# Cache copies as quarters behind the input projection's loads, weight sums behind additions, and a residual put into PSUM

## The chip, the core and the metric

The kernel runs on one core of a Trainium2 chip. TensorE (PE) multiplies matrices and loads its weights on a path of its own (PEld in the profile); VectorE (DVE) and ScalarE (ACT) work on tiles in SBUF and PSUM; GpSimd (POOL) and SyncE (SP) mostly start DMAs here. Each engine has a queue of its own and takes it in order; engines wait for each other by semaphores. The metric is the time of one execution on the device in microseconds (us), lower is better.

## What is computed

One layer of a hybrid decoder, for a prompt of 512 tokens and 8 single sample tokens, 520 columns in all (260 + 260, each half 256 prompt columns and 4 samples), width 1024, float32:

```python
u = rmsnorm(x, g_norm1)
qa, ka, va, qb, kb, vb, rb, glr, ga, gb = split(u @ w_in)        # input projection
oa = dilated window attention(qa, ka, va)                        # prompt, and samples against their caches
ob = gated linear attention(qb, kb, vb, gate(glr))
mix = sigmoid(ga) * (oa @ w_pa) + sigmoid(gb) * (gated ob @ w_pb)
h = x + mix @ w_o
f = square(relu(rmsnorm(h, g_norm2) @ w_up))                     # width 4096
y = rmsnorm(h + f @ w_down, g_final)
```

The new caches of the sample group are outputs too: the old ones, moved by one row, with the new keys and values behind them. The kernel copies the old caches unchanged from DRAM to DRAM; the host puts the new row behind.

## The kernel before

Every product has three passes, since PE multiplies in a rounded format: high part of the weights by high part of the data, high by low, low by high. A weight panel (128 output columns, 1024 inputs, 512 KB) is loaded by SP into a tile raw, ACT rounds it to whi (L138), and DVE subtracts to get wlo (L139); split_piece does both for four k-tiles at a time. While panel i runs, panel i + 1 is split and panel i + 2 loaded.

The program is one straight line. Outside the FFN, Tile's scheduler orders each engine's queue from dependences and an estimate of when things are ready. In the FFN the order is written out: `act`, `add` and `stt` go through `turn` (L119), which chains every instruction of ACT and DVE behind the last one, matmuls are chained by `behind`, and `load` (L86) chains all loads that SP starts. An instruction that waits there holds up all that stands behind it on its engine.

Stages: input projection (58 panels of w_in, `panel_mms` L272, with attention and linear attention filled in between the matmuls), w_pa, w_pb, w_o, and from L1521 the FFN in four quarters of the hidden width. A quarter is four up pairs and, in the first three, four down pairs; `pair_mm` (L203) does one pair. The last quarter's down product is done panel by panel at the end, in two column ranges, 280 and 240 (L1600 to L1647), each with its final norm.

A pair makes a 2 x 2 block product (two panels, two halves of the columns) by seven products instead of eight, in the manner of Strassen and Winograd: P1, P5, P6, P3, P7, P2, P4, each 12 matmuls of 128 x 260. P1 and P2 use plain weights, P5 and P7 use differences of weights (tile sums, made by a load and an accumulating load of POOL, L114 and L115), P6 and P3 use tile s, which `pair_sums` (L146) makes with two DVE additions from sums and raw, and P4 uses the last quarter block (tile rb, `load_rest`). The data side has sums as well (tiles Th/Tl, FT and the second halves of hh and fh). P1, P6, P7 and P4 add up in one PSUM bank x, P5 and P3 in e; P2 adds to a copy of P1 in a. P4 can therefore start only when DVE has read x after P7.

Which work of the next pair stands where in the queues is set by `lead(i, step)`: step 0 makes the sums s, steps 1 to 3 split weights. The results of a pair go on in the next one: `then` of `up_pair` (L1209) gets the names T0, T1, T2 at the start, after P1 and after P5 of the next pair and makes ReLU, square, split and data sums there. `down_pair` (L1282) adds a pair's results into dd, on DVE (in the first quarter the first ones are ACT copies).

`extras` (L1547) puts small work into the down pairs: the squares of h in the first quarter (reloaded from the DRAM copy Hd), in the second the mean square (r2: four ones-matmuls and rv on DVE at P1 of the first down pair, four reciprocals of 130 columns), in the third dd times rv and then the residual, by an accumulating DMA of POOL from Hd into dd (L1578). `pace` (L339) starts the cache copies on POOL, one of 1024 rows (1 MB) a call, each behind a matmul; there are 42 in self.copies, the last 16 for ca3v.

Of the kernel before, what the change touches and what calls it, by code (L numbers as in the profile page):

```python
# [47 lines left out]
class Build:  # L48
# [114 lines left out]
    def lead(self, i, step):  # L163

        if self.panels[i][1] != PAIR:
            if step in (1, 2):
                self.split_panel(i, (4 * step - 4,))
        elif step == 0:
            self.pair_sums(i)
        else:  # L170
            self.pair_piece(i, *{1: ("P1",), 2: ("P6", "P5"), 3: ("P7",)}[step])

    def split_panel(self, i, parts=(0, 4)):
# [6 lines left out]
        if self.panels[i][1] == PAIR:  # L180
            for step in range(3):
                self.lead(i, step)
            return
# [19 lines left out]
    def pair_mm(self, acts, then):  # L203
# [15 lines left out]
        if before:  # L219
            before("T0")  # L220
        self.load_panel(i + 2)
        for n, o, start, end in seq:
# [11 lines left out]
            if n == "P1":  # L234
                if before:
                    before("T1")
            elif n == "P5":
                if before:
                    before("T2")
                if "P7" not in self.ready[i]:  # L240
                    self.pair_piece(i, "P7")
                self.pair_piece(i, "P4" if first else "P2")
                if pair:
                    self.lead(i + 1, 0)
# [7 lines left out]
            elif n == "P7":  # L252
                if not last:
                    self.lead(i + 1, 2)
# [5 lines left out]
            if n == "P2" and pair and not then(n + " ends"):  # L260
                self.lead(i + 1, 3)
        if pair:
            self.later = lambda n: then(n, a, e, x)
        else:
            for n in ("T0", "T1", "T2"):
                then(n, a, e, x)
# [5 lines left out]
    def panel_mms(self, xh, xl, m, pool=None):  # L272
# [6 lines left out]
        if i + 2 < len(self.panels):  # L279
            self.load_panel(i + 2)  # L280
        if i + 1 < len(self.panels):
# [875 lines left out]
    def up_pair(self, p, work, k, fh, fl, T, copies, rv):  # L1157
# [51 lines left out]
        def then(n, a=None, e=None, x=None):  # L1209
# [27 lines left out]
            elif n == "P2 ends":  # L1237
                return end
# [6 lines left out]
            elif n == "T0":  # L1245
# [15 lines left out]
            elif n == "T1":  # L1261
# [4 lines left out]
                else:  # L1266
                    split(4, v["t"])
                    if T:
                        high(0)
            elif n == "T2" and T:  # L1270
                if end:
                    high(2)
                    self.add(fl[:, k + 4], v["t"], fh[:, k + 4].bitcast(F32), op=ALU.subtract)
                    low(2)
                else:
                    high(1)
                    high(2)
                    for n in range(3):
                        low(n)
        return then  # L1280

    def down_pair(self, k, dd, qd, also):  # L1282
# [14 lines left out]
        def then(n, a=None, e=None, x=None):  # L1297
# [11 lines left out]
            elif n == "P4":  # L1309
                self.pace(1)  # L1310
            elif n == "T0":
                put(1, one, x, -1)
# [3 lines left out]
    def run(self):  # L1316
# [26 lines left out]
        for n in ("a1k", "a1v", "a2k", "a2v", "a3k", "a3v"):  # L1343
# [3 lines left out]
            for x in range(pieces):  # L1347
                f = lambda t: t[x * st:(x + 1) * st].rearrange("(a b) c -> a (b c)", a=16)
                self.copies.append((f(o), f(i)))
        self.rate, self.tiny_rate, self.groups_ready = 0, 2, 1  # L1350
# [125 lines left out]
        with pool("late") as p:  # L1476
# [70 lines left out]
            def extras(qd, k):  # L1547
# [3 lines left out]
                def also(n):  # L1551
# [10 lines left out]
                    elif qd == 1:  # L1562
                        if n == "P1" and k == 0:
# [8 lines left out]
                        elif n == "P4":  # L1572
                            c = slice(65 * k, 65 * k + 130)
                            self.turn("DVE", nc.vector.reciprocal(rv[:, c], rv[:, c]))
                    elif n in ("P4", "T0"):
                        x = k + (n == "T0")
                        self.add(dd[:, x], dd[:, x], rv, op=ALU.mult)
                        nc.gpsimd.dma_start(dd[:, x], Hd[:, x], accum_op=ALU.add)  # L1578
                return also

            for qd in range(4):
                n0 = len(self.panels) - KT
                for k in range(4):
                    if qd == 3 and k == 3:
                        self.wdst[n0] = [p.tile([P, KT, P], F32R, tag="sums", name="lw", bufs=3) for _ in range(2)]
                    if qd + k == 0:
                        self.later = lambda n: (list(self.sums_left), low()) if n == "T1" else None
                    self.pair_mm(acts, self.up_pair(p, work, k, fh, fl, T if qd < 3 else None, k % 2 or qd == 3,
# [11 lines left out]
            for j, cc in enumerate((slice(0, JC), slice(JC, NT))):  # L1600
                n = cc.stop - cc.start
                for k in range(KT):
# [6 lines left out]
                    ps = self.bank("mps")[:, :n]  # L1609
                    for kk in (0, 1, 2, 4, 5, 6, 3, 7):  # L1610
                        for x, (w, u) in enumerate(self.passes(self.split[i], kk, fh, fl)):
                            self.last = nc.tensor.matmul(ps, w, u[:, kk, cc], start=(kk == 0 and x == 0),  # L1612
                                                         stop=(kk == KT - 1 and x == 2))
# [185 lines left out]
```

## Time and profile before

| what | us |
|---|---|
| median of 3 runs (896.15 to 899.48) | 898.85 |
| the profiled execution | 898.83 |
| its span in the profile | 897.1 |
| PE busy | 870.5 |
| DVE busy | 659.1 |
| ACT busy | 473.3 |

The profile is of one execution. A stretch of the trace is named by its start and end in us from the start of the span. "Busy" is the time in which at least one instruction of the engine runs; matmuls overlap, so two that follow each other closely count once. The granted clock is the share of PE's full clock, and the DMA share is the mean busy share of the 16 DMA engines. In the timeline a row has start, length, engine, line, operation, tiles (out<-in) and shapes, and in brackets how long the engine stood idle before and what ended the wait by the trace. Of several things waited for, the one that came last is named, and it can be the wrong one.

### The profile page before, as it was taken

The numbers are of one execution on the slowest core, as the hardware profiler recorded it, in microseconds if no ns is written. First come the engines' busy times: TensorE is split into PE (matmuls) and PEld (weight loads), VectorE is DVE, ScalarE is ACT, GpSimd is POOL, SyncE is SP. The second block draws the span as 40 slices with busy tenths as digits, with TensorE's granted clock in tenths as the row PEclk, the third lists the DMA queues.
The fourth block names the chain that finished last, engine by engine and source line by source line (L and its number), as shares of the span: only waits on it lengthen the run. The fifth ranks groups of instructions, "written<-read, shape, count | busy, mean of one in ns | idle before, by whom it ended". The sixth has DMA issues, their size and how long they took to land.

```text
span 897.1 us, 19539 instructions
## 1 busy us (share of the span) xinstructions
PE 870.5 (97%) x7818; PEld 847.2 (94%) x7818; DVE 659.1 (73%) x1333; ACT 473.3 (53%) x989; POOL 118.8 (13%) x171
## 2 busy tenths in 40 slices
PE   9999999999999999999999999999989998998995
PEld 8999999999999999999999999899989998998995
DVE  6877566775947849695755778977998798887843
ACT  6233424453736545364533558867864585456732
POOL 1110000001200302101001211111111111231000
PEclk9999999999999999999999999999999999999998
DMA  7476465324545534225797967799778877998531
GB/s 256 125 269 206 133 212 200 109 73 147 181 151 171 187 128 142 77 72 195 280 380 285 334 227 210 226 310 317 241 198 236 278 229 211 240 298 291 194 122 69
DMA packets 52323, 184.14 MB, mean 205 GB/s; under 512 B 6588, under 2 KB 11716, under 8 KB 50408
## 3 DMA queue, kind: packets, MB, share of 16 engines
q1 hardware_dynamic: 37432, 104.26, 33.4%
q0 software_dynamic: 14512, 78.14, 29.1%
q8 instruction: 61, 1.00, 0.4%
q10 hardware_dynamic: 288, 0.49, 0.2%
q14 instruction: 30, 0.25, 0.1%
HBM read 167.01 MB, written 56.30 MB: 249 GB/s over the span
## 4 chain that ended last, share of the span: by engine, by line
PE 84%; DMA 5%; DVE 5%; ACT 3%; issue 1%; SPq 0%; DVEq 0%; ACTq 0%; POOLq 0%
PE mps L299 48%; PE mps L227 21%; PE mps L1612 5%; DMA sums<-in_w_up 4%; ACT t L128 1%; PE lev L894 1%; PE mps L465 1%; ACT whi L128 1%; PE sps L640 1%; DVE s L131 1%; DVE fl L131 1%; PE pvp L673 1%; DVE wlo L131 1%; PE gpo L1003 1%; PE gpu L1007 1%
## 5 line engine op out<-in xcount | busy, mean ns | idle before, releaser
L299 PE MATMUL mps<-uh,whi 128*128 128x260 f32 x896 | 255.9, 286 | 0.0
L299 PE MATMUL mps<-ul,whi 128*128 128x260 f32 x896 | 255.8, 286 | 0.0
L299 PE MATMUL mps<-uh,wlo 128*128 128x260 f32 x896 | 255.3, 285 | 0.0
L128 ACT ACTIVATE whi<-raw 128x512 fp32r<-128x512 f32 (+1 forms) x210 | 128.8, 619 | 180.4 <-PE mps L299 146.7
L131 DVE TENSOR_TENSOR wlo<-raw,whi 128x512 fp32r<-128x512 f32 (+1 forms) x210 | 141.5, 677 | 58.7 <-ACT whi L128 57.5
L299 PEld LDWEIGHTS mps<-uh,wlo 128*128 128x128 f32 x896 | 168.7, 188 | 2.1 <-issue 1.5
L299 PEld LDWEIGHTS mps<-ul,whi 128*128 128x128 f32 x896 | 168.7, 188 | 1.2 <-issue 0.3
L299 PEld LDWEIGHTS mps<-uh,whi 128*128 128x128 f32 x896 | 168.7, 188 | 1.1 <-issue 0.7
L227 PE MATMUL mps<-Th,whi 128*128 128x260 f32 x256 | 74.0, 289 | 9.6 <-ACT whi L128 9.5
L227 PE MATMUL mps<-Tl,whi 128*128 128x260 f32 x256 | 72.9, 285 | 0.1
L227 PE MATMUL mps<-Th,wlo 128*128 128x260 f32 x256 | 72.8, 284 | 0.0
L227 PE MATMUL mps<-hl,whi 128*128 128x260 f32 x240 | 68.1, 284 | 0.0
L227 PE MATMUL mps<-hh,whi 128*128 128x260 f32 x240 | 68.1, 284 | 0.0
L227 PE MATMUL mps<-hh,wlo 128*128 128x260 f32 x240 | 67.7, 282 | 0.0
L227 PEld LDWEIGHTS mps<-Th,whi 128*128 128x128 f32 x256 | 48.7, 190 | 12.1 <-ACT whi L128 11.3
L227 PE MATMUL mps<-fh,whi 128*128 128x260 f32 x192 | 54.9, 286 | 0.3 <-ACT whi L128 0.3
L227 PE MATMUL mps<-fl,whi 128*128 128x260 f32 x192 | 54.8, 286 | 0.0
L227 PE MATMUL mps<-fh,wlo 128*128 128x260 f32 x192 | 54.5, 284 | 0.0
L128 ACT ACTIVATE whi<-s 128x1024 fp32r<-128x1024 f32 x28 | 29.7, 1060 | 40.2 <-DVE s L131 25.4
L227 PEld LDWEIGHTS mps<-Tl,whi 128*128 128x128 f32 x256 | 48.7, 190 | 0.3 <-DVE Tl L131 0.3
L227 PEld LDWEIGHTS mps<-Th,wlo 128*128 128x128 f32 x256 | 48.8, 191 | 0.0
L1612 PE MATMUL mps<-fh,lw 128*128 128x280 f32 (+1 forms) x256 | 47.3, 285 | 0.4 <-ACT fh L128 0.4
(385 smaller groups left out, 2144.7 us busy)
## 6 DMA issues: line engine op xcount, KB each, us to landing
raw<-in_w_in SPq DMA_DIRECT2D x55, 512.0 KB, 4.3
raw<-in_w_down SPq DMA_DIRECT2D x20, 512.0 KB, 5.3
sums<-in_w_up SPq DMA_DIRECT2D x16, 512.0 KB, 7.9
sums<-in_w_up POOLq DMA_DIRECT2D x16, 512.0 KB, 7.9
raw<-in_w_up SPq DMA_DIRECT2D x16, 512.0 KB, 6.0
sums<-in_w_down SPq DMA_DIRECT2D x12, 512.0 KB
sums<-in_w_down POOLq DMA_DIRECT2D x12, 512.0 KB, 6.1
sx<-in_state SPq DMA_DIRECT2D x8, 512.0 KB, 4.6
```

The costliest lines, as they stand in the source:

```text
L128: return self.turn("ACT", self.nc.scalar.activation(*args, **kw))
L131: return self.turn("DVE", self.nc.vector.tensor_tensor(out, a, b, op=op))
L227: mm = nc.tensor.matmul(o, w[:, k], u, start=(n in ("P1", "P5") and k == 0 and y == 0), stop=(k == 3 and y == 2), skip_group_check=True)
L299: mm = self.nc.tensor.matmul(o[:, :HC], wt, x[:, k, j * HC:(j + 1) * HC], start=(k == 0 and n == 0), stop=(k == kt - 1 and n == 2))
L465: self.last = nc.tensor.matmul(ps[i][:, j, :HC], wt, u[:, k, j * HC:(j + 1) * HC], start=(k == 0 and n == 0), stop=(k == KT - 1 and n == 1))
L640: m = nc.tensor.matmul(pss[hh][:, hp, c], Q[rows, i, b * P:(b + 1) * P], K[rows, i, ks], start=True, stop=True)
L673: m = nc.tensor.matmul(po[64 * hh:64 * hh + 64, hp * P:(hp + 1) * P], v, pTs[hp][:, hh, x], start=(x == first), stop=(x == 1))
L894: m = self.nc.tensor.matmul(out, w, x, start=True, stop=True)
L1003: nc.tensor.matmul(po[:, :256], ST[:, c], V[:, c], start=True, stop=(c == 0))
L1007: nc.tensor.matmul(pu[:, :256], klT[:, c * P:(c + 1) * P], V[:, c], start=True, stop=True)
L1612: self.last = nc.tensor.matmul(ps, w, u[:, kk, cc], start=(kk == 0 and x == 0), stop=(kk == KT - 1 and x == 2))
```

## The change

- **Copies.** Twelve of the 42 copies are taken from the end of the list, cut into four along the bytes of each row, and started by SP, one quarter behind the load that each panel from 10 on starts. The FFN's calls of pace are fewer: one in each down pair but the first of a quarter, and one in the last three up pairs.
- **Order in a pair.** The sums s of the next pair stand behind the additions after P7 and no longer behind P5. The split of P6 comes last (behind P2), that of P5 behind the sums, that of P7 always in its own pair, behind P5. The late work of the pair before is spread over "behind", "behind P1", "behind P5" and "behind P6".
- **Mean square.** r2 and rv move from P1 of the first down pair of the second quarter to P4 of its second pair; the reciprocals go to P1 and P4 of the third and fourth.
- **Residual.** The accumulating DMAs go. In the last stage each panel's part of h is loaded into a tile (tag tr, two buffers). For the first four panels of the first column range DVE adds it to dd; for the other twelve ACT copies it into the PSUM bank before the matmuls, which add to it.

```diff
@@ lead
         else:
-            self.pair_piece(i, *{1: ("P1",), 2: ("P6", "P5"), 3: ("P7",)}[step])
+            self.pair_piece(i, ("P1", "P5", "P6")[step - 1])
@@ split_panel
-            for step in range(3):
+            for step in range(4):
                 self.lead(i, step)
@@ pair_mm
         if before:
-            before("T0")
+            before("behind")
...
-            if n == "P1":
-                if before:
-                    before("T1")
-            elif n == "P5":
-                if before:
-                    before("T2")
+            if before and n in ("P1", "P6", "P3", "P7"):
+                before("behind " + n)
+            if n == "P5":
                 if "P7" not in self.ready[i]:
                     self.pair_piece(i, "P7")
+                if before:
+                    before("behind P5")
                 self.pair_piece(i, "P4" if first else "P2")
-                if pair:
-                    self.lead(i + 1, 0)
...
             elif n == "P7":
+                if pair:
+                    self.lead(i + 1, 0)
                 if not last:
                     self.lead(i + 1, 2)
...
-            if n == "P2" and pair and not then(n + " ends"):
+            elif n == "P2" and pair:
                 self.lead(i + 1, 3)
         if pair:
             self.later = lambda n: then(n, a, e, x)
         else:
-            for n in ("T0", "T1", "T2"):
+            for n in ("behind", "behind P1"):
                 then(n, a, e, x)
@@ panel_mms
             self.load_panel(i + 2)
+        if i >= 10 and self.quarters:
+            self.load(*self.quarters.pop(0))
@@ up_pair
-            elif n == "P2 ends":
-                return end
...
-            elif n == "T0":
+            elif n == "behind":
...
-            elif n == "T1":
+            elif n == "behind P1":
                 if T and end:
                     high(1)
                     low(1)
                     self.act(fh[:, k + 4], v["t"], AF.Copy)
                 else:
                     split(4, v["t"])
-                    if T:
-                        high(0)
-            elif n == "T2" and T:
+            elif T and n == "behind P5":
                 if end:
-                    high(2)
                     self.add(fl[:, k + 4], v["t"], fh[:, k + 4].bitcast(F32), op=ALU.subtract)
-                    low(2)
                 else:
-                    high(1)
-                    high(2)
-                    for n in range(3):
+                    for n in range(2):
+                        high(n)
                         low(n)
+            elif T and n == "behind P6":
+                high(2)
+                low(2)
@@ down_pair
             elif n == "P4":
-                self.pace(1)
-            elif n == "T0":
+                self.pace(k > 0)
+            elif n == "behind":
                 put(1, one, x, -1)
@@ run
+        self.quarters = []
+        for o, i in (self.copies.pop() for x in range(12)):
+            self.quarters += [[t[:, y * t.shape[1] // 4:(y + 1) * t.shape[1] // 4] for t in (o, i)] for y in range(4)]
...
                     elif qd == 1:
-                        if n == "P1" and k == 0:
+                        if n == "P4" and k == 2:
...
-                        elif n == "P4":
-                            c = slice(65 * k, 65 * k + 130)
+                        elif n in ("P1", "P4") and k > 2:
+                            c = slice(130 * (k - 4 + (n == "P4")), 130 * (k - 3 + (n == "P4")))
                             self.turn("DVE", nc.vector.reciprocal(rv[:, c], rv[:, c]))
-                    elif n in ("P4", "T0"):
-                        x = k + (n == "T0")
+                    elif n in ("P4", "behind"):
+                        x = k + (n == "behind")
                         self.add(dd[:, x], dd[:, x], rv, op=ALU.mult)
-                        nc.gpsimd.dma_start(dd[:, x], Hd[:, x], accum_op=ALU.add)
...
-                        self.later = lambda n: (list(self.sums_left), low()) if n == "T1" else None
-                    self.pair_mm(acts, self.up_pair(p, work, k, fh, fl, T if qd < 3 else None, k % 2 or qd == 3,
+                        self.later = lambda n: (list(self.sums_left), low()) if n == "behind P1" else None
+                    self.pair_mm(acts, self.up_pair(p, work, k, fh, fl, T if qd < 3 else None, qd == 3 and k > 0,
                                                     rv if qd == 3 else None))
...
                     ps = self.bank("mps")[:, :n]
+                    h = self.late.tile([P, 3 * HC], F32, tag="tr", name="h", bufs=2)[:, :n]
+                    self.load(h, Hd[:, k, cc])
+                    early = j == 0 and k < 4
+                    if early:
+                        nc.vector.tensor_tensor(dd[:, k, cc], dd[:, k, cc], h, op=ALU.add)
+                    else:
+                        nc.scalar.activation(ps, h, AF.Copy)
                     for kk in (0, 1, 2, 4, 5, 6, 3, 7):
                         for x, (w, u) in enumerate(self.passes(self.split[i], kk, fh, fl)):
-                            self.last = nc.tensor.matmul(ps, w, u[:, kk, cc], start=(kk == 0 and x == 0),
-                                                         stop=(kk == KT - 1 and x == 2))
+                            self.last = nc.tensor.matmul(ps, w, u[:, kk, cc], start=(early and kk == 0 and x == 0),
+                                                         stop=(kk == KT - 1 and x == 2), skip_group_check=True)
```

## The prediction

> **What bounds the kernel now.** The page first: is TensorE (PE) the bound, and how much of the span is it idle?
>
> ```profile
> span 897.1 us, 19539 instructions
> PE 870.5 (97%) x7818; PEld 847.2 (94%) x7818; DVE 659.1 (73%) x1333; ACT 473.3 (53%) x989; POOL 118.8 (13%) x171
> ```
>
> PE works for 97%, so only a wait of PE, or of what PE waits for, can be won. The windows by stage say where those are (stretch in us, its length, busy time of PE, PEld, DVE, ACT, POOL, granted clock, DMA share, GB/s). From 530 on the FFN runs in 28 pairs of panels: per quarter of the hidden width four up pairs, then four down pairs (three quarters), and four up pairs in the last.
>
> ```profile
> 65.00:345.00 280.00, 280.00 (x2724) 268.09 (x2723) 196.68 (x454) 125.89 (x292) 29.55 (x46) 1.00 0.47 160
> 450.00:500.00 50.00, 50.00 (x420) 50.00 (x419) 30.24 (x49) 19.34 (x32) 5.51 (x11) 1.00 0.90 336
> 530.28:574.45 44.17, 41.99 (x339) 40.68 (x338) 38.93 (x72) 35.02 (x76) 4.75 (x5) 1.00 0.59 165
> 574.45:616.12 41.67, 41.29 (x338) 40.49 (x337) 32.90 (x56) 28.80 (x59) 7.07 (x8) 1.00 1.00 316
> 616.12:658.76 42.64, 40.89 (x338) 40.34 (x337) 37.20 (x69) 34.38 (x76) 5.91 (x6) 1.00 0.81 233
> 658.76:703.29 44.53, 42.31 (x342) 41.39 (x341) 37.37 (x69) 20.81 (x37) 7.01 (x8) 1.00 0.75 232
> 703.29:746.60 43.31, 41.16 (x339) 40.43 (x338) 37.40 (x70) 33.06 (x73) 5.91 (x6) 1.00 0.86 249
> 746.60:792.31 45.71, 43.43 (x338) 42.21 (x337) 38.41 (x71) 20.80 (x37) 11.67 (x14) 0.96 0.87 249
> 792.31:839.60 47.29, 43.76 (x351) 43.40 (x350) 34.06 (x57) 30.39 (x62) 7.09 (x9) 0.96 0.87 271
> ...
> 596.01:606.06 10.05, 10.05 (x86) 10.05 (x85) 7.59 (x13) 6.64 (x14) 1.76 (x2) 1.00 1.04 341
> 636.88:647.82 10.94, 10.28 (x87) 10.10 (x85) 10.06 (x20) 9.08 (x22) 1.75 (x2) 1.00 0.87 274
> 658.76:672.58 13.82, 11.60 (x91) 11.06 (x90) 12.03 (x24) 7.99 (x16) 1.76 (x2) 1.00 0.79 253
> 746.60:761.60 15.00, 12.72 (x87) 11.89 (x85) 12.30 (x25) 7.98 (x16) 2.19 (x3) 0.89 0.80 258
> ```
>
> Before 530 PE is busy without a break, even where the DMA engines are at 0.90. A pair without a wait takes 10.05 us (596.01 to 606.06), four take 40.2. Over that lie: up pairs 3.97, 2.44 and 3.11; down pairs 1.47, 4.33 and 5.51; last up pairs 7.09, of which 14 matmuls of the next stage at 10.05/84 us each are work (1.68), so 5.41. Together 26.2 us: all that can be won.
>
> What PE waits for is in its timeline (start, length, idle before and releaser):
>
> ```profile
> 646.31 0.36 PE L227 MATMUL mps<-Th,whi 128*128 128x260 f32 x1 [0.66 <-ACT whi L128]
> 668.18 0.36 PE L227 MATMUL mps<-FT,whi 128*128 128x260 f32 x1 [2.22 <-DVE dd L131]
> 755.67 0.49 PE L227 MATMUL mps<-FT,whi 128*128 128x260 f32 x2 [2.20 <-DVE dd L131]
> 824.93 0.56 PE L227 MATMUL mps<-Th,whi 128*128 128x260 f32 x1 [3.00 <-ACT whi L128]
> ```
>
> The first is P4 of an up pair. The name given is ACT's whi, but P4 adds into the bank x, which DVE must first have read (t<-mps,P). The DVE and ACT rows of this and the next pair:
>
> ```profile
> 643.22 0.68 DVE L131 TENSOR_TENSOR s<-sums,raw 128x512 f32<-128x512 f32 x1
> 643.93 0.69 DVE L131 TENSOR_TENSOR s<-s,raw 128x512 f32<-128x512 f32 x1
> ...
> 649.71 0.43 DVE L131 TENSOR_TENSOR fl<-t,fh 128x260 fp32r<-128x260 f32 x1 [0.56 <-ACT fh L128]
> ...
> 654.16 0.68 DVE L131 TENSOR_TENSOR s<-sums,raw 128x512 f32<-128x512 f32 x1
> ...
> 655.49 0.68 DVE L131 TENSOR_TENSOR wlo<-rb,whi 128x512 fp32r<-128x512 f32 x1
> ...
> 656.69 0.75 DVE L131 TENSOR_TENSOR t<-mps,P 128x260 f32<-128x260 f32 x2
> 657.37 1.21 DVE L131 TENSOR_TENSOR wlo<-s,whi 128x1024 fp32r<-128x1024 f32 x1
> ```
>
> ```profile
> 644.72 1.06 ACT L128 ACTIVATE whi<-s 128x1024 fp32r<-128x1024 f32 x1 [1.33 <-DVE s L131]
> 645.68 0.61 ACT L128 ACTIVATE whi<-sums 128x512 fp32r<-128x512 f32 x1
> ...
> 646.86 0.37 ACT L128 ACTIVATE t<-mps 128x260 f32<-128x260 f32 x1
> 647.26 0.64 ACT L128 ACTIVATE t<-t 128x520 f32<-128x520 f32 x1
> ...
> 648.73 0.64 ACT L128 ACTIVATE t<-t 128x520 f32<-128x520 f32 x1
> 649.27 0.40 ACT L128 ACTIVATE fh<-t 128x260 fp32r<-128x260 f32 x1
> ```
>
> The two weight sums s stand ahead of t in DVE's queue; t starts at 656.69 and P4 follows. But DVE is busy 10.06 of the 10.94 us: it has as much work in such a pair as PE. That decides how much the new order can give.
>
> **Part 1, order in the up pairs.** No instruction goes or comes; s,s move behind the two additions t, the split of P6 behind P2, the split of P7 from the pair before to behind P5, and the T pieces a step later. I follow the loop that results. From fl (649.71) to t (656.69) are 6.98 us; s,s leave (654.16 to 655.49, 1.33) and the P7 split comes in (0.60, half a 1.21 split): 6.25. From t to the end of s: 0.68 for the additions (656.69 to 657.37) and 1.40 for s,s (643.22 to 643.93 + 0.69). Then 0.10 until ACT starts whi<-s (644.62 to 644.72), 0.96 until ACT takes the next one, 0.40 for the ReLU (646.86 to 647.26), 0.54 for the square (648.73 to 649.27), 0.44 from fh to fl (649.27 to 649.71). Sum 10.77 us a pair against 10.94: DVE waits for ACT's P6 split, which waits for DVE's s. So it gives 0.17 a pair, not the 0.89. The first up pair of a quarter comes out of light down pairs and is free; the second uses up DVE's lead (I take 0.25 over), the others 0.72 each: 1.7 a quarter, and 1.0 more in the first, whose start isn't changed. 6.1 in place of 9.52, **gain 3.4**. Ends: 9.52 (DVE no limit) and 0 (loop as before).
>
> **Part 2, the first down pair.** 3.77 and 4.95 us over 10.05 in the second and third quarters. The wait of 2.2 at P7 is for an addition to dd:
>
> ```profile
> 667.61 0.42 DVE L131 TENSOR_TENSOR dd<-mps,dd 128x260 f32<-128x260 f32 x1
> L1566 PE MATMUL r<-acc,ones x4: 381/382/383, 660.5 to 661.1; 128*128 128x260 f32 x4
> ```
>
> It stands behind s,s (1.33) and, in the second quarter, behind rv on DVE; both move away. What is late next: the last up pair's s,s, P6 split and rest now run into the down pair. By the same rows low(0) ends about 3.6 after its P1 starts where P5's last k-tile wants it at 2.7; behind that FT is 0.4 late, the dd addition 0.65, small ones 0.35: 2.3 in all. In the first quarter ACT does these copies: 1.5, as now. The four matmuls of r2 (0.75, 660.5 to 661.1 and their length) are only moved two pairs on, where nothing waits for rv before the next quarter. The later down pairs lose their 0.19 each, since s,s no longer stand ahead of dd. So 1.5 + 3.05 + 2.3 = 6.85 in place of 11.31, **gain 4.5**. Ends: 9 (all covered) and 0.
>
> In this sum lies the clock. The window from 746.60 shows it at 0.89, that is 0.11 x 15.00 = 1.65 us lost, right after the wait of 2.2; after the equal wait at 668 nothing was lost. Waits cut into pieces below 1 us should not set it off. [...]
>
> **Part 3, last up pairs and the copies.** PE's 3.00 at 824.93 is the same P4 wait, with s late itself:
>
> ```profile
> 813.03 1.21 POOL L115 DMA_DIRECT2D sums<-in_w_up  x1 [8.92 <-ACT t L128]
> ...
> 821.82 0.69 DVE L131 TENSOR_TENSOR s<-sums,raw 128x512 f32<-128x512 f32 x1 [3.97 <-DMA sums<-in_w_up]
> ```
>
> The accumulating load was issued at 813.03 and landed at 821.8. Two things take this wait away, each alone: s now stands behind t, and P6 of the next pair, its first user, comes three groups of twelve matmuls (4.3 us) later than P4; and the DMA load falls, by 12 copies of 1 MB and the eight accumulations into dd. There DVE has no T work and is busy 34.06 of 47.29, so no loop binds. 5.4 becomes 0.3, **gain 5.1** (with the clock's 0.04 x 47). Ends: 5.4, and 2 if another load is late.
>
> The copies cost time elsewhere: 48 quarters on SP, one behind each weight load of panels 10 to 57. They wait for nothing themselves; queued behind each on SP are the next weight load (two panels ahead of its use) and, between them, the small loads of the attention.
>
> ```profile
> q0 software_dynamic: 14512, 78.14, 29.1%
> ```
>
> At 0.291 x 897.1 / 78.14 = 3.3 us of all engines per MB, 12 MB (1024 rows of 1 KB a copy) are 40 us, spread over some 330 (an estimate from the 48 panels between about 70 and 400): share 0.47 to about 0.6, under the 0.90 where PE is unbroken. I take **-0.5**; ends 0 and -12 (a rival).
>
> **Part 4, residual.** Eight POOL accumulations go; sixteen loads h come on SP, four DVE additions and twelve ACT copies into PSUM. Until now dd was complete before this stage; now each h must have landed before its addition or copy. There DVE and ACT have spare time, panel after panel of PE (some 3 us each) covers a load, and two buffers let one run ahead. The first loads stand on SP behind the last weight loads, which wait for buffers; there an addition that waits for h would hold up the weight splits queued behind it on DVE. **-0.5**; ends 0 and -18 (below).
>
> Sum: 3.4 + 4.5 + 5.1 - 0.5 - 0.5 = 12.0. The profiled execution took 898.83 (1.7 around its span), the median is 898.85: **886.8 us**.
>
> **Rivals.**
> *PSUM copies stand in line (slower).* The rows of one panel of the last stage:
>
> ```profile
> 858.11 0.45 DVE L1618 TENSOR_TENSOR dd<-mps,dd 128x280 f32<-128x280 f32 x1 [1.68 <-PE mps L1612]
> ...
> 841.22 5.30 ACT L128 ACTIVATE lw<-raw 128x512 fp32r<-128x512 f32 x10
> ...
> 858.59 0.44 ACT L1620 ACTIVATE t<-dd 128x280 f32<-128x280 f32 x1 [2.08 <-DVE dd L1618]
> ```
>
> If ACT takes the copy of h for panel k+1 behind the square of panel k, PE idles from the end of panel k over addition and square (858.11 to 859.03) and a copy of some 0.37, with handovers 1.5 us, 12 times: 18 us, 904.8. It decides as soon as ACT's queue holds that order. Against it: ACT ran the weight splits of five panels (lw, 841.22) before the first panel's square, though later in the code, so the queue is ordered by what is ready, and four banks let the copy run ahead. 0.10.
> *Copies hurt the projection.* The attention's small loads share SP's queue; a late one stops PE, which runs in order. 48 quarters with 0.15 to 0.25 us each give 7 to 12 back: 894 to 899. For it: share 0.47 with large loads in bursts. Against: no wait at 0.90. 0.13. [...] No row here has quarters.
> *DVE is no limit.* If DVE's splits overlap better than the loop says, parts 1 and 2 give up to 9 us more: 878 to 882. Against it: 10.06 of 10.94 busy. 0.12.
> *The order gives nothing.* Loop and first down pair stay as they are; only part 3 is won: 893 to 896. 0.10.
>
> **How the numbers follow.** Forecast 0.55 (883 to 891), rivals 0.10, 0.13, 0.12, 0.10. The range 878 to 898 holds all but the slower rival and the top of the second. A measurement of this kernel tells 0.5% (4.5 us) from no change: faster 0.55 + 0.12 + some 0.10 of the middle cases = 0.77, same 0.12, slower 0.11.
>
> **What would show it.** Right: up pairs two to four of a quarter near 10.8 us and DVE busy some 10.1 in them; no idle of PE over 1 us in the first down pairs or after 790; clock 1.00 up to the tail; PE unbroken before 530. Wrong, with another cause than mine: up pairs at 10.05 (no loop), PE idle between the panels of the last stage (copies in line), or gaps between 70 and 400.

## The result and the profile after

| | before | after |
|---|---|---|
| median on the same chip, 4 runs each | 897.84 (896.15 to 899.48) | 890.99 (890.13 to 891.26) |
| span of the profiled execution | 897.05 | 889.48 |

The ratio is 0.9922, 95% interval 0.9900 to 0.9945: 0.8% faster. Predicted was 886.8, the forecast's own range 883 to 891. First the page of the changed kernel:

```profile
span 889.5 us, 19573 instructions
PE 868.9 (98%) x7818; PEld 845.5 (95%) x7818; DVE 661.0 (74%) x1337; ACT 475.0 (53%) x1001; POOL 106.0 (12%) x151
```

PE does the same 7818 instructions, and the span is 7.6 us shorter. The windows of the changed kernel, cut at the first matmul of each group of four pairs (columns as in the prediction), say where:

```profile
335.00:420.00 85.00, 85.00 (x998) 83.00 (x998) 63.72 (x150) 41.14 (x97) 14.01 (x19) 1.00 0.44 151
420.00:445.00 25.00, 24.74 (x198) 24.05 (x197) 19.03 (x40) 16.84 (x26) 2.34 (x5) 1.00 0.60 208
...
531.99:574.67 42.68, 41.41 (x338) 40.62 (x337) 37.70 (x71) 34.34 (x75) 4.21 (x4) 1.00 0.63 166
574.67:616.80 42.13, 41.27 (x338) 40.44 (x337) 33.39 (x56) 28.34 (x58) 5.89 (x6) 1.00 0.88 267
616.80:658.71 41.91, 40.97 (x338) 40.44 (x337) 37.41 (x70) 34.76 (x77) 5.37 (x5) 1.00 0.75 211
658.71:702.31 43.60, 42.44 (x343) 41.38 (x341) 37.72 (x70) 20.29 (x37) 5.83 (x6) 1.00 0.75 209
702.31:744.21 41.90, 40.96 (x339) 40.43 (x337) 37.58 (x71) 33.53 (x74) 5.33 (x5) 1.00 0.74 211
744.21:786.85 42.64, 41.50 (x339) 40.60 (x337) 38.35 (x72) 20.28 (x37) 5.85 (x6) 1.00 0.75 213
786.85:829.20 42.35, 42.35 (x356) 42.35 (x354) 35.46 (x58) 30.94 (x64) 4.03 (x5) 1.00 0.72 237
829.20:881.07 51.87, 48.42 (x379) 47.20 (x377) 27.76 (x60) 26.71 (x63) 0.49 (x1) 0.97 0.33 110
...
833.00:840.00 7.00, 6.92 (x39) 6.69 (x40) 6.59 (x13) 6.99 (x15) 0.00 (x0) 0.76 0.33 108
```

Two windows of the kernel before, to lay beside them:

```profile
839.61:887.89 48.28, 47.25 (x383) 46.10 (x381) 26.13 (x56) 23.60 (x51) 1.46 (x3) 1.00 0.34 122
335.00:420.00 85.00, 85.00 (x996) 82.94 (x994) 62.94 (x149) 41.40 (x98) 12.61 (x18) 1.00 0.33 114
```

In the last up pairs PE is busy for all of 42.35 us (40.2, and 18 matmuls of the last stage done ahead: 18 x 10.05/84 = 2.15), and the clock no longer drops at 756 and at 825. Yet the FFN starts 1.71 later, and the last stage takes 51.87, where before it took 48.28; the clock drops there instead.

All kernels of this study are laid side by side in one table: us over 40.2 a group of four pairs, from the start times of PE's rows. "Projection" is the time from its first matmul to the start of the FFN against that of before (the first matmul itself comes up to 1.2 us earlier or later from run to run, with no tie to the kernel). "Last stage" runs from the end of the last pair to the ones-matmul of the final norm and includes the matmuls done ahead (14 or 18). Each ratio is to runs of before on the same chip.

| kernel | median | ratio to before, interval | projection | up pairs | down pairs | last up pairs | last stage |
|---|---|---|---|---|---|---|---|
| before | 897.84 | 1 | 0 | 9.50 | 11.33 | 5.41 | 49.96 |
| after | 890.99 | 0.9922 (0.9900 to 0.9945) | 1.74 | 5.90 | 7.76 | 0 | 54.02 |
| x1_no_quarters | 887.15 | 0.9864 (0.9849 to 0.9879) | -0.08 | 5.90 | 7.71 | 0 | 52.74 |
| x2_no_residual | 887.34 | 0.9862 (0.9847 to 0.9877) | 2.00 | 5.87 | 7.74 | 0 | 50.28 |
| x3_order_only | 887.43 | 0.9862 (0.9847 to 0.9877) | 0.41 | 5.88 | 7.03 | 2.23 | 50.29 |
| x7_copies_only | 895.34 | 0.9952 (0.9935 to 0.9969) | 2.55 | 8.88 | 11.28 | 2.78 | 50.24 |
| x4_early_h | 887.69 | 0.9870 (0.9839 to 0.9902) | 1.89 | 5.92 | 7.77 | 0.28 | 51.00 |
| x5_late_lows | 885.25 | 0.9842 (0.9810 to 0.9874) | 1.93 | 0.60 | 8.08 | 0 | 53.57 |
| x8_mean_square_first | 890.38 | 0.9896 (0.9861 to 0.9930) | 1.70 | 5.90 | 7.05 | 0 | 52.52 |
| x9_best | 880.73 | 0.9794 (0.9756 to 0.9832) | 0.28 | 0.56 | 7.34 | 0.28 | 50.92 |
| x10_few_rows (the changed kernel again) | 890.02 | 0.9898 (0.9880 to 0.9915) | 2.09 | 5.90 | 7.80 | 0 | 53.35 |
| x11_earlier | 889.76 | 0.9898 (0.9875 to 0.9922) | 2.06 | 5.92 | 7.80 | 0 | 53.17 |
| x12_one_row (one run) | 889.15 | | 1.11 | 5.94 | 7.76 | 0 | 53.52 |

From before to after: 3.60 + 3.57 + 5.41 gained in the pairs, 1.74 lost in the projection and 4.06 in the last stage, 0.75 gained behind it: 7.53 of the 7.57 between the spans. For the 0.75 (9.16 to 8.41) no reason was found: the engines' rows behind the ones-matmuls take 4.99 in both, so it lies behind the last of them, and x3 has 8.87 there, x7 8.43. x10 shows how well such numbers repeat: 0.7 us in the last stage, 0.35 in the projection, under 0.1 in the pairs.

What PE waits for in the changed kernel's FFN, from its timeline:

```profile
646.47 0.36 PE L227 MATMUL mps<-Th,whi 128*128 128x260 f32 x1 [0.43 <-DVE t L131]
...
662.35 0.39 PE L227 MATMUL mps<-hl,whi 128*128 128x260 f32 x1 [0.57 <-DVE hl L131]
666.78 0.47 PE L227 MATMUL mps<-FT,whi 128*128 128x260 f32 x2 [0.53 <-DVE dd L131]
...
832.21 0.39 PE L1618 MATMUL mps<-fh,lw 128*128 128x280 f32 x1 [2.72 <-ACT fh L128]
```

P4 (646.47) now names DVE's t, as the prediction read it, where before the row named ACT's whi. The waits of 2.2 in the down pairs have become pieces under 0.6. The new one is at 832.21. Behind it stand these rows of SP, DVE and ACT:

```profile
824.09 0.42 SPq L87 DMA_DIRECT2D h<-Hd  x1
```

```profile
826.51 0.42 DVE L131 TENSOR_TENSOR t<-mps,P 128x260 f32<-128x260 f32 x1
830.42 0.45 DVE L1613 TENSOR_TENSOR dd<-dd,h 128x280 f32<-128x280 f32 x1 [3.49 <-DMA h<-Hd]
830.79 0.69 DVE L131 TENSOR_TENSOR t<-t,rv 128x520 f32<-128x520 f32 x1
```

```profile
831.52 0.64 ACT L128 ACTIVATE fh<-t 128x520 fp32r<-128x520 f32 x1 [3.13 <-DVE t L131]
...
846.10 0.42 ACT L1626 ACTIVATE t<-dd 128x280 f32<-128x280 f32 x1
846.43 0.39 ACT L1615 ACTIVATE mps<-h 128x280 f32<-128x280 f32 x1
```

The first h is issued at 824.09 behind the weight loads and is there at 830.4. The addition that uses it stands in DVE's queue ahead of the last up pair's own products with rv (830.79). DVE stands 3.49 us for a tile of 140 KB that the products don't need; their input t was ready on ACT at 828.39, so they start 2.4 late. fh comes late, and the first panel of the last stage with it. The copies of h into PSUM (L1615) run between the others on ACT; PE names them nowhere.

### The profile page after: what moved, and what is told of

It is laid out like the page before. It is cut to its first block, busy times and chain, and to the rows that moved or that the text cites. A ratio compares the mean times of both kernels' runs of the same rounds, so it can differ in the third digit from the quotient of the medians.

```text
span 889.5 us, 19573 instructions
## 1 busy us (share of the span) xinstructions
PE 868.9 (98%) x7818; PEld 845.5 (95%) x7818; DVE 661.0 (74%) x1337; ACT 475.0 (53%) x1001; POOL 106.0 (12%) x151
## 4 chain that ended last, share of the span: by engine, by line
PE 81%; ACT 8%; DVE 7%; issue 2%; DMA 1%; SPq 0%; DVEq 0%; ACTq 0%
PE mps L300 47%; PE mps L227 18%; PE mps L1618 5%; DVE wlo L131 3%; ACT t L128 3%; ACT whi L128 2%; DVE fl L131 1%; PE lev L895 1%; PE mps L466 1%; PE sps L641 1%; ACT fh L128 1%; PE pvp L674 1%; PE gpo L1004 1%; PE gpu L1008 1%; PE ptp L658 1%
## 5 line engine op out<-in xcount | busy, mean ns | idle before, releaser
L128 ACT ACTIVATE whi<-sums 128x512 fp32r<-128x512 f32 x56 | 35.1, 628 | 39.6 <-PE mps L227 39.6
```

Of the source, the lines that this page charges most:

```text
L128: return self.turn("ACT", self.nc.scalar.activation(*args, **kw))
```

## The experiments: one part at a time

**x1_no_quarters**: the changed kernel with the twelve copies back on POOL.

```diff
-        for o, i in (self.copies.pop() for x in range(12)):
-            self.quarters += [...]
-                self.pace(k > 0)
+                self.pace(1)
-  ... T if qd < 3 else None, qd == 3 and k > 0,
+  ... T if qd < 3 else None, k % 2 or qd == 3,
```

> The changed kernel with the copies as before (all 42 on POOL, none behind the projection's loads); order, mean square and residual as changed. My theory: the order alone keeps late sums from PE, and the quarters cost the projection 1.7 us. So the FFN's first matmul is back at 530.3 (532.0 with the quarters), the last up pairs still have no wait of PE over 1 us even where sums land late, and the time is about 889.3 (888.5 to 890.5). Rival, the copies' relief of the DMA is what took the wait of 3.00 away: it comes back at the last up pairs, 3 to 5 us, time 892 to 894.

The projection is as long as before (-0.08), and with all copies back in the FFN the last up pairs still have no wait:

```profile
786.00:826.46 40.46, 40.46 (x340) 40.46 (x338) 33.76 (x55) 30.16 (x63) 4.49 (x6) 1.00 0.81 270
```

So the moved copies cost 1.7 to 2.1 and bring nothing here: 0.9864 against 0.9922 (and 0.9898 of the repeat), intervals apart. The time is 2.9 to 3.8 lower, more than the projection gives; the last stage is 0.6 to 1.3 shorter as well. There the first h lands 5.3 after its issue in place of 6.3 (6.2 in the repeat), so DVE waits 2.47 for it and PE 1.70 in place of 2.72 (2.55). Why it lands sooner was not tried.

**x2_no_residual**: the changed kernel with the accumulating DMAs of before.

```diff
+                        nc.gpsimd.dma_start(dd[:, x], Hd[:, x], accum_op=ALU.add)
-                    h = self.late.tile([P, 3 * HC], F32, tag="tr", name="h", bufs=2)[:, :n]
-                    self.load(h, Hd[:, k, cc])
...
-                            ... start=(early and kk == 0 and x == 0),
+                            ... start=(kk == 0 and x == 0),
```

> The changed kernel with the residual as before (eight accumulating DMAs of POOL into dd in the third quarter, no loads of h in the last stage). My theory: DVE's wait of 3.49 for the first h is what costs the last stage about 2.9 us, so DVE has no wait for a DMA between 820 and 835, PE's gap of 3.01 at its first panel shrinks to about 0.7, and the time is about 888.1 (887.3 to 889). Rival, the accumulations crowd out the sums of the last quarter again: gaps of PE of 2 us or more after 786, time 890 to 892.

The windows of the last stage, and of the 7 us where the changed kernel had the clock at 0.76:

```profile
828.31:876.44 48.13, 46.75 (x379) 45.62 (x377) 25.87 (x55) 23.57 (x51) 0.49 (x1) 1.00 0.20 71
831.00:838.00 7.00, 7.00 (x55) 6.85 (x55) 6.95 (x14) 5.77 (x12) 0.00 (x0) 1.00 0.42 125
```

48.13 in place of 51.87, clock 1.00, no long wait, and still none in the last up pairs. The new residual costs 3.7 us (3.1 against the repeat), about half of it in the clock: 0.24 x 7.00 = 1.7.

**x3_order_only**: x1's and x2's edits and, as in x8 below, the mean square at its old place; what is left is the order in a pair.

> The kernel before with the order of the pairs alone changed: copies, mean square and residual as before. My theory, the order does nearly all: up pairs at 10.73, first down pairs some 2.3 over, no wait at the last up pairs though copies and accumulations are all back, FFN start at 530.3; time about 886.5 (885.5 to 888). Rival, without relief the sums land too late even for the new order: a wait of 2 us or more in the last quarter, time 889 to 891.

Order alone gives as much as all of x1 or x2, but in the last up pairs 2.23 of 5.41 come back. DVE's timeline and the window of these pairs:

```profile
814.12 0.69 DVE L131 TENSOR_TENSOR s<-sums,raw 128x512 f32<-128x512 f32 x1 [1.00 <-DMA sums<-in_w_up]
```

```profile
784.12:828.70 44.58, 42.92 (x356) 42.51 (x354) 36.45 (x59) 30.40 (x64) 6.33 (x8) 1.00 0.93 294
```

With the copies and the accumulations both in this stage the DMA share is 0.93 (0.72 after, 0.81 in x1), and s waits for its accumulating load again. Less of either, as in x1 and x2, ends the wait. But the share alone does not decide it. x2's window of these pairs has nearly the same share, and s has no wait in it:

```profile
785.97:828.31 42.34, 42.34 (x355) 42.34 (x354) 36.16 (x59) 30.95 (x65) 6.08 (x8) 1.00 0.92 286
```

Why the load lands late in x3 and not in x2 stays open.

**x7_copies_only**: the kernel before with the quarters and the changed pace calls, nothing else.

> The kernel before with the twelve copies alone moved. My theory: FFN start 1.7 us later, up pairs at 10.94 and the waits of 2.2 as before, since they are DVE's queue; the wait of 3.00 in the last quarter gets smaller as the DMA load falls but does not go, time 894 to 899. Rival, DMA load is what makes s late: that wait goes altogether, time 893 to 894.

The counterpart: less DMA in the old order. Window and DVE row of its last up pairs:

```profile
793.43:838.09 44.66, 42.33 (x352) 41.97 (x350) 33.79 (x56) 30.26 (x62) 5.93 (x8) 1.00 0.87 265
```

```profile
821.75 0.69 DVE L131 TENSOR_TENSOR s<-sums,raw 128x512 f32<-128x512 f32 x1 [2.59 <-DMA sums<-in_w_up]
```

s waits 2.59 for its load, where before it waited 3.97. PE's wait falls from 3.00 to 1.62, and the clock stays at 1.00 behind it, so 2.63 of 5.41 are gained, and 2.55 are lost in the projection.

## The experiments: the three things that did not come as forecast

**x4_early_h** tests the reading of the wait at 832: the first two parts of h are loaded ahead of the third of the last up pairs and added to dd ahead of the fourth.

```diff
+                    if qd == 3 and k == 2:
+                        hs = [self.late.tile([P, 3 * HC], ...)[:, :JC] for _ in range(2)]
+                        for x in range(2):
+                            self.load(hs[x], Hd[:, x, :JC])
+                    if qd == 3 and k == 3:
+                        for x in range(2):
+                            self.add(dd[:, x, :JC], dd[:, x, :JC], hs[x])
...
+                    if j or k > 1:
                         h = ...
```

> The changed kernel with the first two parts of h loaded one pair earlier (ahead of the third of the last up pairs) and added to dd ahead of the last one; nothing else moved. My theory: the residual costs the last stage 3.7 us (51.9 from the last P4 to the final ones-matmuls, 48.1 without it) only because DVE waits 3.49 for the first h, with ReLU products queued behind it, and because the gap of PE that follows sets the clock to half for 3.4 us. So that stage takes 48.1 to 49.2, its half-clock window goes, and the time is 2.7 to 3.7 lower than the changed kernel's 890.99. Rival, the twelve ACT copies and the other loads cost too: the stage stays over 50.

On DVE the products of the last up pair come right after ACT, with no wait for a load:

```profile
828.51 0.70 DVE L131 TENSOR_TENSOR t<-t,rv 128x520 f32<-128x520 f32 x1 [1.49 <-ACT t L128]
```

The clock stays at 1.00, and the last stage takes 51.00 in place of 54.02 (48.85 without the 18 matmuls done ahead, where 48.1 to 49.2 was expected). It is the place of the first loads and their additions that cost the time, not the fourteen other loads or the copies into PSUM; 0.7 over x2 is left, no more than a repeat moves.

**x5_late_lows** tests the loop between DVE and ACT that the prediction followed. In the changed kernel one pass of it reads on DVE:

```profile
645.90 0.76 DVE L131 TENSOR_TENSOR t<-mps,P 128x260 f32<-128x260 f32 x2
646.58 0.68 DVE L131 TENSOR_TENSOR s<-sums,raw 128x512 f32<-128x512 f32 x1
647.29 0.69 DVE L131 TENSOR_TENSOR s<-s,raw 128x512 f32<-128x512 f32 x1
...
649.11 1.23 DVE L131 TENSOR_TENSOR wlo<-s,whi 128x1024 fp32r<-128x1024 f32 x1 [0.53 <-ACT whi L128]
650.37 0.43 DVE L131 TENSOR_TENSOR fl<-t,fh 128x260 fp32r<-128x260 f32 x1
...
656.63 0.76 DVE L131 TENSOR_TENSOR t<-mps,P 128x260 f32<-128x260 f32 x2
```

t to t is 10.73: 2.08 to the end of s, 2.39 to fl, 6.26 to the next t. In the middle DVE stands for 0.53 while ACT makes whi from s. If this loop is the bound, work taken from between fl and t and put into that hole makes the pair shorter with nothing removed. Two of the three "low" subtractions go there:

```diff
-                    for n in range(2):
-                        high(n)
-                        low(n)
+                    high(0)
+                    high(1)
+                    low(1)
             elif T and n == "behind P6":
                 high(2)
-                low(2)
+                if end:
+                    low(2)
+            elif T and n == "late" and not end:
+                low(0)
+                low(2)
...
                     self.lead(i + 1, 2)
+                if before:
+                    before("late")
```

> The changed kernel with two low parts of the data sums (low(0) and low(2), 0.34 each on DVE, of the first three up pairs of a quarter) moved from behind P5 and P6 to behind the next pair's weight sums and P5 split. My theory: up pairs two to four take 10.73 because of the loop from s over ACT's split of s, the data sums and t back to s. The two moved pieces leave the loop and fill DVE's wait for ACT, so these pairs take 10.15 to 10.35, and the three quarters gain 2.5 to 4 us together, first down pairs included. Rival, DVE's total work binds (10.1 busy of 10.73, no order helps): 10.6 to 10.73, time as the changed kernel within 0.7.

One pair of the third group and its DVE rows:

```profile
636.06:646.12 10.06, 10.06 (x86) 10.06 (x85) 9.96 (x20) 9.25 (x21) 1.19 (x1) 1.00 0.73 187
```

```profile
643.99 0.69 DVE L131 TENSOR_TENSOR wlo<-sums,whi 128x512 fp32r<-128x512 f32 x1
644.59 0.42 DVE L131 TENSOR_TENSOR hl<-t,hh 128x260 fp32r<-128x260 f32 x1
644.93 0.42 DVE L131 TENSOR_TENSOR fl<-tr,fh 128x260 fp32r<-128x260 f32 x1
645.27 1.22 DVE L131 TENSOR_TENSOR wlo<-s,whi 128x1024 fp32r<-128x1024 f32 x1
```

The two subtractions fill the hole, wlo<-s follows with no idle time, and the pair takes 10.06: PE's own time. The up pairs fall from 5.90 to 0.60 over. DVE is busy for 9.96 of 10.06 and still not the bound, so its amount of work was not what held the pair; the rival falls. I had expected a gain of 2.5 to 4, first down pairs included, and got 5.0: 5.3 in the up pairs, less 0.3 in the down pairs.

**x8_mean_square_first**: the changed kernel with r2, rv and the reciprocals where they were before.

```diff
-                        if n == "P4" and k == 2:
+                        if n == "P1" and k == 0:
...
-                        elif n in ("P1", "P4") and k > 2:
-                            c = slice(130 * (k - 4 + (n == "P4")), 130 * (k - 3 + (n == "P4")))
+                        elif n == "P4":
+                            c = slice(65 * k, 65 * k + 130)
```

> The changed kernel with the mean square and the reciprocals where they were before (P1 of the first down pair of the second quarter, P4 of each). My theory: in the first down pair PE waits for hl anyway, so the four matmuls are free there and cost 0.75 where they were moved to: the four down pairs of the second quarter take 2.7 over 40.2 in place of 3.4, time 0.7 lower. Rival, rv on DVE delays the dd addition: 3.4 or more.

The four matmuls of r2 in x8 and then in the changed kernel, first and last start:

```profile
L1566 PE MATMUL r<-acc,ones x4: 381/382/383, 659.3 to 660.0; 128*128 128x260 f32 x4
```

```profile
L1566 PE MATMUL r<-acc,ones x4: 382/382/383, 681.2 to 681.9; 128*128 128x260 f32 x4
```

In x8 they run in the first down pair, just where PE has to wait for hl a little later (662.35 above; x8 has no such wait), so they cost little: the down pairs of this quarter lose 2.67, those of the third quarter, without r2, 2.44. Two pairs on PE waits for nothing, and the quarter loses 3.39. All down pairs lose 7.05 in place of 7.76. The time itself (890.38) lies within the spread of the other runs, so this 0.7 is shown by the trace alone. x8's last stage is 1.5 shorter than after's: PE's wait there is 2.23, and behind it the clock stays at 1.00.

**x10_few_rows, x11_earlier, x12_one_row** ask why the projection is longer: is it the bytes of the quarters, or the order in which the scheduler places small work around them?

```diff
-  ... self.quarters += [[t[:, y * t.shape[1] // 4:(y + 1) * t.shape[1] // 4] ...
+  ... self.quarters += [[t[:1, y * t.shape[1] // 4:(y + 1) * t.shape[1] // 4] ...
```

This is x12; x10 has `t[:16, ` there, and x11 only `if i >= 2` in place of `if i >= 10` at the place that starts a quarter.

> The 48 quarters stand on SP at the same places, but each copies 16 rows in place of 1024, so hardly any bytes move (the rest of the twelve caches is not copied). Projection, from its first matmul to the start of the FFN, was 1.7 us longer with the quarters than before (0.7 near 330, 1.0 between 420 and 450). Theory, order: the quarters change the order in which the scheduler puts the small work behind the matmuls, and PE loses the time there, whatever the bytes; then the projection stays 1.5 to 2 us longer and the time is that of the changed kernel, 890 to 891.5. Rival, bytes: the copies take DMA time from the weight and attention loads; then the projection falls back to within 0.4 of before and the time is 889 to 889.8. The FFN is the same in both (last stage 51 to 52).

> The quarters stand behind the loads of panels 2 to 49 in place of 10 to 57, whole. If the bytes near the end of the projection cost the 1.0 us between 420 and 450, it goes, since no copy then runs beside the loads of the last eight panels: projection 0.7 us longer than before, time about 890. If the order is the cause, the loss moves or stays as the new order has it, between 0 and 2.5 us, with no tie to the place of the copies. The FFN is as in the changed kernel.

> The caches' tiles have 16 rows, so the kernel that cut them to 16 rows was the changed kernel once more. Here each of the 48 quarters copies 1 row of 16 (16 KB in place of 256; the other rows of the twelve caches are not copied); they stand on SP behind the same loads, but the scheduler, which sees shorter copies, orders some of the small work otherwise. Theory, order: the projection's length follows the order, not the bytes; as this order is a third one it may be anything from 0.1 shorter to 2 longer than before, and only a value of 1 or more speaks for the theory. Rival, bytes: 1/16 of the bytes leaves at most 0.15 us. A value below 0.5 leaves both open.

x10 tells nothing of the question: the tiles have 16 rows, so `t[:16]` cuts nothing off, and it is a repeat of the changed kernel. x11 does tell something. SP's rows of the last quarter, in the changed kernel and then in x11, and x11's windows:

```profile
412.47 3.61 SPq L87 DMA_DIRECT2D out_ca3v<-in_ca3v  x1
```

```profile
354.25 0.52 SPq L87 DMA_DIRECT2D out_ca3v<-in_ca3v  x1
```

```profile
335.00:420.00 85.00, 84.80 (x996) 82.66 (x994) 63.67 (x150) 40.76 (x97) 14.25 (x19) 1.00 0.38 127
420.00:445.00 25.00, 24.74 (x200) 24.09 (x199) 18.66 (x40) 17.00 (x27) 2.04 (x4) 1.00 0.63 213
```

The last quarter is issued 58 us earlier, and fewer bytes move from 335 to 420 (127 GB/s; 151 after). The loss is the same (2.06; 2.09 in x10).

Where it arises is seen when the starts of PE's matmuls are laid beside those of before. In after, x2, x4, x5, x7, x8, x10 and x11, PE falls behind by 0.7 between 329 and 334, and by 0.9 more by 435; in before, x1, x3, x9 and x12 at neither place. The quarters' bytes are not needed for that. From 330 to 340 the DMA share is 0.40 after and 0.42 before, and the 0.9 stands in x11 too, where no quarter is issued behind 354. What the eight kernels share is the sequence of PE's rows ahead of the FFN. Before, x1, x3 and x9 share another, which differs from it in 550 of 5068 rows, all between 240 and 439.

x12, with 1/16 of the bytes, has the sequence of before, but for two rows that change places at 275; it is not the third order that was expected. It has neither of the two losses. Its 1.11 is lost elsewhere, 0.6 by 277 and 0.5 by 460, the first with this wait of PE:

```profile
272.13 0.66 PE L605 MATMUL vps<-ident,vt 128*128 128x128 f32 x4 [0.41 <-DVE vt L597]
```

Waits at this line come in other runs of either sequence too (0.58 in x7, 0.10 in x9), and so they make up part of what a repeat moves. So about 1.6 of the loss goes with the order of PE's rows, at places where the bytes make no difference. That the order alone does it is argued from these places: no run has whole quarters in the old order. Why the scheduler orders so when SP has the quarters wasn't tried.

**x9_best** puts x1, x4, x5 and x8 together on the changed kernel: no quarters, h early, the lows late, the mean square first.

> All that the runs so far speak for: order as changed with the two low parts moved, mean square as before, copies as before on POOL, residual into PSUM with the first two parts of h loaded early. By my theory the gains add: 1.7 of the projection, 0.7 of the mean square, about 3 of the last stage, about 3 of the loop, so 881.5 to 884 against the changed kernel's 890.99, ratio to before 0.980 to 0.985. Rival, what one part gives another takes back (the copies' load makes sums or h late again): 885 or more.

880.73 (879.87 to 881.4), ratio 0.9794 (0.9756 to 0.9832): 18.5 below the kernel before on its chip (899.20). The gains add up, to 0.8 below the expected range. From the FFN's start to the final norm's ones-matmul x9 takes 340.52 (529.35 to 869.87), after 349.08 (531.99 to 881.07): 8.56 less. By the table 5.34 of it is in the up pairs (x5 alone: 5.30), 3.10 in the last stage (x4 alone: 3.02) and 0.42 in the down pairs, where x8's 0.7 and x5's -0.3 meet, less 0.28 ahead of the last stage, as in x4.

## Why the prediction came out as it did

Faster by more than 0.5% was the likeliest case, and the time lies in the range, at the upper end of the forecast's own. Of its five terms three were right and the two small ones were several times too small. About six tenths of the forecast gain were measured, and that the time is still inside is in part luck: 890.99 stands at the very end of 883 to 891, and it owes 0.75 to the stretch behind the last stage, which no part of the change explains. Two of the forecast's own signs failed, both at the residual: PE stood idle for over 1 us after 790 (2.72), and the clock fell ahead of the tail (0.76 from 833 to 840).

| step | predicted | measured (before to after) |
|---|---|---|
| order in the up pairs | 3.4 | 3.60 |
| first down pairs | 4.5 | 3.57 |
| last up pairs | 5.1 | 5.41 |
| copies in the projection | -0.5 | -1.74 |
| residual in the last stage | -0.5 | -4.06 |
| behind the last stage | 0 | 0.75 |
| sum | 12.0 | 7.53 |

- **Up pairs: right, by its mechanism.** Its loop gave 10.77 a pair; it is 10.73, and its pieces stand in the rows: 2.08 as predicted, 2.39 for 2.44, 6.26 for 6.25. x5 shows that it is this loop, and that DVE's 10.06 busy us a pair, on which the prediction also leaned against its rival "DVE is no limit", bound nothing. That rival's 878 to 882 is where x9 ends, but through another order than the changed kernel's.
- **Down pairs: right, 0.9 too much.** The waits of 2.2 and the clock's loss went. By quarters it is 1.93 for 1.5, 3.39 for 3.05 and 2.44 for 2.3. The 0.75 of r2 was counted (3.05 is 2.3 + 0.75), but as a cost that only moves; x8 shows that at its old place, where PE waits anyway, the quarter loses 2.67. The largest miss is the first quarter's 0.43. It was taken as unchanged, though its late work moved too; no run takes that apart.
- **Last up pairs: right in sum, half wrong in its reason.** "Two things take this wait away, each alone" doesn't hold: order alone leaves 2.23 (x3), less DMA by the quarters alone 2.78 (x7); no run has both reliefs, copies and accumulations, in the old order. Order with either relief leaves 0 (x1, x2). The accumulations into dd, gone by the residual's edit, would have been relief enough, and the twelve copies need not have moved.
- **Copies: the size and the mechanism failed.** The prediction looked for bytes on the DMA engines and for small loads late on SP. Its share was right: from 65 to 345 it rose from 0.47 to 0.56, for a forecast of about 0.6. But the loss goes with another order of PE's rows, which the step did not consider, at places where the bytes make no difference (x11).
- **Residual: the mechanism was named and priced at nearly nothing.** "There an addition that waits for h would hold up the weight splits queued behind it on DVE" is what happens at 826.93, save that the products of the last up pair stand behind it too, and the next panel needs those. The step counted spare time of the engines, where one row in the order of DVE's queue decided. It left out PE's wait for that row, 2.72 where before it was 0.38, and the clock's 1.7 behind it: 4.04 of the 4.06. The rival "PSUM copies stand in line" did not happen: ACT ran them ahead, and PE waits for one of them only in x8, for 0.27.

## What to carry to other kernels

Where two in-order engines feed each other, write down the loop with the hole in it before counting busy time: a stage may be bound with every engine idle at times, and moving 0.7 us of work into the hole can free it with nothing removed (x5: 5.3 us over twelve pairs, without one instruction less). Something new that waits for a DMA must not stand in an in-order queue ahead of work that the critical engine needs next; load it one step earlier (x4: 3.02 us of the last stage, where DVE had stood 3.49 for h). To put it behind that work was not tried. And small work was nearly free where the bound engine waited (0.2 us in x8), and cost 0.95 where that engine didn't wait (in the changed kernel), so "only moved" needs a look at both places (x8).

## What the runs showed of the hardware

In x7 one wait of PE of 2.22 us cost 1.7 us beyond its length, and another of 2.22 cost nothing beyond it. They stand in the first down pairs of the second and third quarter; PE's rows, and the windows behind them:

```profile
669.99 0.48 PE L227 MATMUL mps<-FT,whi 128*128 128x260 f32 x2 [2.22 <-DVE dd L131]
...
756.83 0.63 PE L227 MATMUL mps<-FT,whi 128*128 128x260 f32 x2 [2.22 <-DVE dd L131]
```

```profile
670.00:677.00 7.00, 7.00 (x58) 7.00 (x59) 5.63 (x10) 2.91 (x6) 1.19 (x1) 1.00 0.57 191
...
756.80:763.80 7.00, 6.97 (x45) 7.00 (x46) 5.22 (x10) 1.96 (x3) 1.20 (x1) 0.76 0.54 190
```

Behind the first the granted clock stays at 1.00 and 58 matmuls run in 7 us, behind the second it is 0.76 and 45 run: 1.7 us lost, as before at the same places and as in the changed kernel at 833 after 2.72 idle. Each time the granted clock is 0.50 for 3.41 us. The windows of x7 and x1:

```profile
756.98:760.39 3.41, 3.41 (x17) 3.41 (x18) 1.63 (x5) 1.15 (x2) 0.00 (x0) 0.50 0.57 173
```

```profile
829.94:833.35 3.41, 3.41 (x16) 3.29 (x15) 3.41 (x7) 3.41 (x8) 0.00 (x0) 0.50 0.38 107
```

Between 20 and 870 the traces of the thirteen kernels have fourteen gaps of PE over 1 us. Nine have such a stretch at half clock beside them: 1.70 (x1), 2.20, 2.21, 2.22, 2.28, 2.50, 2.55, 2.72 and 3.00. Five have none: 1.14, 1.62, 2.22, 2.22 and 2.23 (x8). So in these traces, from 1.62 to 2.28 us, the length of the gap alone does not decide it.

A stretch of 3.41 us at 0.50 loses 3.41 x 0.50 = 1.7 us, which agrees with the window of x7 (0.24 x 7.00 = 1.7). Why one gap of 2.22 has such a stretch beside it and another has none, no run shows. What is left of the waits of 2.2 in the changed kernel's down pairs, pieces under 0.6, costs no clock (1.00).
